# A hybrid decoder step: seven products in the FFN's down projection, 295 GB/s in the list scheduler's costs, one kind of weight sum kept as float32

## The chip, the cores and the metric

The kernel runs on one core of one Trainium2 chip. The metric is the device time of one execution in microseconds; the kernel before takes 2984.06 us, the median of three runs (2978.11 to 2984.43). Engines are named as in the profile: PE is TensorE, PEld its weight loads, DVE VectorE, ACT ScalarE, POOL GpSimd, SP the engine that issues DMAs.

## The reference

One layer of a hybrid decoder for a prompt of 2048 tokens and eight single decode tokens, in float32: a mixer (a convolution group beside gated DeltaNet), cross-attention into 256 memory tokens, and the dense FFN, to which the change belongs:

```python
def swiglu(h, w_gate, w_up, w_down):
    return (jax.nn.silu(h @ w_gate) * (h @ w_up)) @ w_down
...
x = x + swiglu(rms_norm(x, norm_ffn), w_gate, w_up, w_down)
```

The model width is 1024, the hidden width 2816.

## The kernel before

Channels lie on the 128 partitions and tokens run along the free axis. The prompt is cut into four blocks of 512 tokens; block 2 also carries the eight decode tokens in its FFN (520 columns, two halves of 260). The hidden width is 22 chunks of 128, called f; the model width is 8 chunks, called m.

Every float32 product is made of three matmuls. A weight tile w holds the value rounded to fp32r in its first half and the rest in its second; so do activations. `three` issues high x high, high x low and low x high into the same PSUM bank. The rounding is a ScalarE copy, the rest a subtraction on GpSimd or VectorE ("split"): `WS.split` does it for weights, choosing GpSimd unless it is behind.

The gate and up projections of a chunk f are already done in seven products (`product`: Q1, P5, P6, Q2, Q3, Q7, P4) of half a block's tokens each, in the banks fx, fy and fz, from four sums of weight tiles besides the tiles themselves. The sums are made once, split, and parked in DRAM (`sums`) as split pairs, 512 KB each; blocks 1 to 3 load them straight into a weight tile, without a split. `ff_split` multiplies the two branches (ffu, ffs) and splits the result into a tile ff.

The down projection (`down(g, j)`) takes a pair of chunks f and two of the eight m: for each m a bank dn gets 2 x 3 matmuls over all 512 tokens (in block 2 two banks of 260), and one VectorE addition brings the bank to the residual tile x. A pair and four j are one weight load of 256 KB and one split each.

`ffn_steps` lists the steps of one block, `ffn_plan` turns them into the order of weight loads and splits, `ffn` walks through them and records the instructions. Behind block 2's products the down projections of three pairs (`HOLD`) are kept back and stand between block 2's last product and block 3's first (`rest`): the bridge, in which block 3's norm is made.

What is recorded is not what is issued. `Tape.order` sorts all instructions again with a list scheduler: it keeps an own clock for each engine, with a cost for each kind (`Tape.cost`), latencies between engines (`LAT`), the buffers of each pool, and issues what is ready, the earliest needed first. Each engine then executes its own queue in that fixed order. A DMA's cost there is its bytes over a rate. Pools that matter here: six weight tiles (`NW`), eleven raw tiles (`NRAW`), 28 float32 tiles (`NT2`), 22 split activations (`NACT`), and for these products the PSUM banks of the tags mm, cv and o.

The line that the profile names is that of a recording helper for all instructions (L469), so rows are told apart by tile names: dn the down projection's banks, fx, fy, fz those of the gate and up products, ffu and ffs their evacuated parts, ff the split hidden tile, x the residual, w a weight tile, raw what was loaded for it, op the split operands of the FFN.

## Time and profile before

| | before |
|---|---|
| median of 3 runs | 2984.06 us |
| the profiled execution: time | 2980.41 us |
| its span | 2978.7 us |
| TensorE busy | 2922.9 us, 98% |
| weight loads | 2601.6 us, 87% |
| VectorE, ScalarE, GpSimd busy | 66%, 46%, 50% |
| DMA, mean of the span | 199 GB/s |

The span is the time from the first to the last instruction of the execution that was profiled, and lies 1.7 us below that execution's device time. A busy matmul in the profile is pipelined: the next begins before it ends, so a group's duration of one is longer than its pace. The pace is read from the chain of waits, in which each piece ends where the next begins. The FFN of block 1 runs from about 1770 to 2123 us, that of block 2 from 2270 to 2580, the bridge to 2625, and block 3's FFN to 2955.

### The profile page before, as it was taken

Reading aid. Unit: us, or ns where it says so; the run is one execution under the profiler, and the core shown is the slowest. Engines: PE = TensorE matmul, PEld = TensorE weight load, DVE = VectorE, ACT = ScalarE, POOL = GpSimd, SP = SyncE. Lnnn points to the kernel's source line nnn. Section 1 sums busy time; section 2 is a strip of 40 time slices with the busy share of each in tenths; the row PEclk is TensorE's granted clock in tenths of the full one; section 3 lists DMA queues with packets and bytes.
Section 4 is the critical chain, followed back from the end, with each engine's and each line's share of the span. In section 5 each row is a group of like instructions: output and inputs, shape, how many; then the busy total and the mean of one; then the engine's idle time right before and its main releaser. Section 6 shows DMA issues by size and latency. Waiting matters only on the chain.

```text
span 2978.7 us, 53399 instructions
## 1 busy us (share of the span) xinstructions
PE 2922.9 (98%) x18972; PEld 2601.6 (87%) x18972; DVE 1975.7 (66%) x3973; ACT 1373.8 (46%) x2854; POOL 1478.0 (50%) x1407
## 2 busy tenths in 40 slices
PE   9999999999999998999999999999999999999998
PEld 7999878887888887999988789988888999999997
DVE  8757798987684867957689874433775444664345
ACT  6543556455764545635554553333453232333233
POOL 3544545776656454548875124445503444344444
PEclk9999999999999999999999999999999999999999
DMA  6533435877773435766778767867526666676663
GB/s 213 158 96 106 130 110 163 262 239 255 225 224 112 140 101 162 253 190 222 256 251 273 252 210 244 262 227 241 176 93 233 208 223 214 213 245 216 223 220 134
DMA packets 361962, 593.89 MB, mean 199 GB/s; under 512 B 54016, under 2 KB 148544, under 8 KB 361680
## 3 DMA queue, kind: packets, MB, share of 16 engines
q1 hardware_dynamic: 361696, 590.47, 61.4%
q8 instruction: 151, 2.47, 0.3%
q14 instruction: 115, 0.94, 0.1%
HBM read 476.65 MB, written 114.27 MB: 198 GB/s over the span
## 4 chain that ended last, share of the span: by engine, by line
PE 76%; DVE 7%; issue 5%; DMA 5%; POOL 5%; ACT 2%; SPq 0%; POOLq 0%; DVEq 0%; ACTq 0%
PE dn L469 14%; PE hd L469 11%; PE fy L469 11%; PE rg L469 9%; PE fx L469 7%; PE fz L469 7%; PE sc L469 5%; POOL w L469 3%; DVE cacc L469 3%; PE pu L469 2%; PE glua L469 2%; PE glub L469 2%; DMA w<-sums 1%; PE pch L469 1%; PE po L469 1%
## 5 line engine op out<-in xcount | busy, mean ns | idle before, releaser
L469 POOL TENSOR_TENSOR w<-raw,w 128x512 fp32r<-128x512 f32 x709 | 957.4, 1361 | 877.7 <-ACT w L469 830.3
L469 ACT ACTIVATE w<-raw 128x512 fp32r<-128x512 f32 x912 | 568.6, 631 | 827.7 <-PE fx L469 175.0
L469 PE MATMUL dn<-ff,w 128*128 128x512 f32 (+2 forms) x2688 | 514.2, 347 | 0.8 <-DVE ffs L469 0.6
L469 PEld LDWEIGHTS dn<-ff,w 128*128 128x128 f32 x2688 | 422.8, 188 | 61.5 <-issue 0.8
L469 PE MATMUL fy<-op,w 128*128 128x256 f32 (+1 forms) x3168 | 426.5, 282 | 3.6 <-DMA w<-sums 3.5
L469 PEld LDWEIGHTS fy<-op,w 128*128 128x128 f32 x3168 | 398.6, 188 | 8.9 <-DVE ffu L469 2.8
L469 PE MATMUL hd<-hT,w 128*128 128x512 f32 (+2 forms) x1920 | 397.7, 357 | 8.2 <-ACT w L469 6.0
L469 DVE SCALAR_TENSOR_TENSOR cacc<-cu,cw,cacc 128x512 f32<-128x512 f32 x480 | 359.5, 749 | 16.1 <-ACT cacc L469 8.2
L469 PEld LDWEIGHTS hd<-hT,w 128*128 128x128 f32 x1920 | 304.3, 189 | 52.5 <-ACT w L469 6.8
L469 DVE TENSOR_TENSOR x<-dn,x 128x512 f32<-128x512 f32 (+1 forms) x448 | 254.4, 572 | 139.4 <-PE dn L469 136.1
L469 PE MATMUL fz<-op,w 128*128 128x256 f32 (+1 forms) x2112 | 287.4, 282 | 0.2 <-DMA w<-sums 0.2
L469 PE MATMUL fx<-op,w 128*128 128x256 f32 (+1 forms) x2112 | 284.7, 282 | 0.3
L469 PEld LDWEIGHTS fx<-op,w 128*128 128x128 f32 x2112 | 267.2, 189 | 6.9 <-issue 1.2
L469 PEld LDWEIGHTS fz<-op,w 128*128 128x128 f32 x2112 | 265.3, 188 | 2.2 <-issue 1.3
L469 POOL TENSOR_TENSOR sqj<-sqj,sqj 128x512 f32<-128x512 f32 (+1 forms) x98 | 134.1, 1368 | 265.5 <-ACT sqj L469 263.3
L469 DVE TENSOR_TENSOR w<-raw,w 128x512 fp32r<-128x512 f32 x203 | 180.0, 892 | 69.4 <-ACT w L469 66.0
L469 PE MATMUL rg<-pT,w 128*128 128x512 f32 x768 | 191.5, 401 | 8.1 <-ACT cres L469 7.9
L469 PE MATMUL sc<-w,hT 128*128 128x512 f32 x768 | 189.4, 398 | 2.4 <-DVE w L469 1.3
L469 PE MATMUL rg<-catS,w 128*128 128x512 f32 (+1 forms) x960 | 188.2, 352 | 1.8 <-ACT jn L469 1.7
L469 DVE TENSOR_TENSOR ffu<-fy,ffu 128x256 f32<-128x256 f32 (+1 forms) x176 | 74.4, 423 | 167.2 <-PE fy L469 167.2
L469 PEld LDWEIGHTS rg<-catS,w 128*128 128x128 f32 x960 | 154.4, 188 | 27.0 <-ACT jn L469 2.5
L469 PEld LDWEIGHTS rg<-pT,w 128*128 128x128 f32 x768 | 142.0, 190 | 40.7 <-ACT cres L469 8.3
(378 smaller groups left out, 4101.2 us busy)
## 6 DMA issues: line engine op xcount, KB each, us to landing
w<-sums SPq DMA_DIRECT2D x296, 512.0 KB, 4.5
raw<-in_w_gate_dram SPq DMA_DIRECT2D x192, 256.0 KB, 3.3
sums<-w SPq DMA_DIRECT2D x88, 512.0 KB, 4.1
raw<-in_w_down_dram SPq DMA_DIRECT2D x176, 256.0 KB, 3.0
raw<-in_w_up_dram SPq DMA_DIRECT2D x118, 256.0 KB, 2.9
raw<-in_w_in_dram SPq DMA_DIRECT2D x96, 256.0 KB, 3.1
raw<-in_w_out_dram SPq DMA_DIRECT2D x64, 256.0 KB, 4.3
raw<-wk SPq DMA_DIRECT2D x64, 256.0 KB, 2.9
```

The costliest lines, as they stand in the source:

```text
L469: fn(*args, **kw)
```

## The change

The down projection of the first twenty chunks f in blocks 1 to 3 is done in seven products of half a block's tokens. Two chunks f and two chunks m (now j and j + 4) make a 2 x 2 matrix of weight tiles, two chunks f and two halves of the tokens one of activations; four sums of the weights and four of the activations take the place of the eighth product (`sums_down`, `pair_split`). `downs(g, j)` does two pairs at once: 7 products x 2 pairs x 3 matmuls into three banks, dx, dy and dz, which are added to x after each product and go on accumulating. The last pair of chunks and all of block 0 stay with `down`, with m and the weight layout changed to j and j + 4. Block 1 makes the weight sums from `w_down` (128 columns each, in place in the raw tiles) and parks them in `dsums` as float32; blocks 2 and 3 load them from there, 512 and 384 columns, and split them.

The fourth sum of the gate and up weights (`WHOLE = (3,)`, the tile of Q7) is parked as float32 (256 KB, `sums1`) in place of a split pair (512 KB), and split whenever it is loaded. The list scheduler's DMA cost uses 295 in place of 360 bytes per ns. In block 2 the residual tiles hold the decode tokens beside each half until the last pair. Counted over the whole program, TensorE issues 600 instructions more (17942 before), VectorE 185 (3975), ScalarE 251 (2599), GpSimd 297 (1412) and SP 200 (1948).

```diff
-            return max(size / 360.0, 90.0), False, None
+            return max(size / 295.0, 90.0), False, None
...
+    def ffn_steps_ds(b):
+        steps = []
+        for f in range(NF):
+            if f == 0 or not early:
+                steps.append(("Q1", f))
+            dec = [w for w, (db, f0) in (("w_mq", DEC_Q), ("w_mo", DEC_O)) if db == b and f0 <= f < f0 + KC]
+            steps += [("P5", f), ("P6", f)]
+            steps += [("dec", dec[0], 2 * (f - (DEC_Q if dec[0] == "w_mq" else DEC_O)[1]) + n) for n in range(2) if dec]
+            steps += [("Q2", f), ("Q3", f), ("Q7", f)]
+            units = [[], []]
+            for g in range(NDS - (b == NB - 2)):
+                for j, (df, end) in enumerate(DS_AT):
+                    if f == min(4 * g + 4 + df, NF - 1):
+                        units[end].append(("downs", g, j))
+            early = not units[0] + units[1] and f + 1 < NF
+            if early:
+                steps.append(("Q1", f + 1))
+            steps += units[0] + [("P4", f)] + units[1]
+        if b < NB - 2:
+            steps += [("down", NG - 1, j) for j in range(KC // 2)]
+        return steps
+    def downs_plan(b, g, j):
+        if b > DS_B:
+            for n in range(2):
+                for p in (2 * g, 2 * g + 1):
+                    plan.append(("dsums", "s", (p, j), n))
+            return
+        raws = {}
+        for p in (2 * g, 2 * g + 1):
+            for n in (1, 0):
+                raws[p, n] = plan.raw("dma", "w_down", "h", (p, j), n)
+        for n in range(2):
+            for p in (2 * g, 2 * g + 1):
+                plan.append(("dsums", "s", (p, j), n), raws[p, n])
...
+    WHOLE = (3,)
...
+                elif PROD[st] in WHOLE:
+                    plan.append(ffn_key(st, f), plan.raw("dma", "sums1", "u", f, WHOLE.index(PROD[st])))
+                else:
+                    plan.append(ffn_key(st, f), -1)
...
-            plan.extend(("w_down", "d", g, j) for g in range(NG - HOLD, NG) for j in range(KC // 2))
+            for j in range(KC // 2):
+                downs_plan(b, NDS - 1, j)
+            plan.extend(("w_down", "d", NG - 1, j) for j in range(KC // 2))
...
+                elif kind == "h":
+                    at = b_ * TB // 2
+                    dma(r[:, at : at + TB // 2], src[a][:, at : at + TB // 2], fr)
+                elif kind == "s":
+                    wd = TB - b_ * P
+                    dma(r[:, :wd], src[a[0], a[1], b_, :, :wd], fr)
...
+                if n in WHOLE:
+                    dma(wsrc["sums1"][f, WHOLE.index(n)], r)
+                else:
+                    dma(wsrc["sums"][f, n], t.bitcast(F32))
...
+        def split_down(self, j, k, r, t):
+            _, _, at, n = plan[j]
+            wd = TB - n * P
+            if plan.raws[k][2] == "h" and n == 0:
+                self.sums_down(at, r, self.raw[k - 1])
+            A.activation(out=t[:, 0, :wd], in_=r[:, :wd], func=AF.Copy)
+            self.engine().tensor_tensor(out=t[:, 1, :wd], in0=r[:, :wd], in1=t[:, 0, :wd].bitcast(F32), op=ALU.subtract)
+            self.tiles[j] = t
+            self.sp += 1
+            self.used(k)
+        def sums_down(self, at, r0, r1):
+            (a11, a12, s1, s2), (s3, s4, a22, a21) = ([r[:, n * P : (n + 1) * P] for n in range(4)] for r in (r0, r1))
+            eng = self.engine(2600.0)
+            for out, x, y, op in (
+                (s1, a21, a22, ALU.add), (s2, s1, a11, ALU.subtract), (s3, a11, a21, ALU.subtract), (s4, a12, s2, ALU.subtract)
+            ):
+                eng.tensor_tensor(out=out, in0=x, in1=y, op=op)
+            p, j = at
+            dma(wsrc["dsums"][p, j, 0], r0)
+            dma(wsrc["dsums"][p, j, 1, :, : 3 * P], r1[:, : 3 * P])
...
+        def pair_split(p):
+            (u1, s1), (u2, s2) = prod.pop(2 * p), prod.pop(2 * p + 1)
+            half = lambda t, n: t[:, n * w : (n + 1) * w]
+            yield [u2, s2]
+            V.tensor_tensor(out=u2, in0=u2, in1=s2, op=ALU.mult)
+            V.tensor_tensor(out=half(s2, 1), in0=half(u2, 1), in1=half(u1, 1), op=ALU.subtract)
+            V.tensor_tensor(out=half(u1, 1), in0=half(u1, 1), in1=half(u1, 0), op=ALU.subtract)
+            V.tensor_tensor(out=half(s2, 0), in0=half(u2, 1), in1=half(u1, 1), op=ALU.subtract)
+            V.tensor_tensor(out=half(s1, 0), in0=half(u2, 0), in1=half(s2, 0), op=ALU.subtract)
+            for n, (src, wd) in enumerate(((u1, 2 * w), (u2, 2 * w), (s2, 2 * w), (s1, w))):
+                yield ("act", 1)
+                a = act("fo")
+                A.activation(out=a[:, 0, :wd], in_=src[:, :wd], func=AF.Copy)
+                yield a
+                V.tensor_tensor(out=a[:, 1, :wd], in0=src[:, :wd], in1=a[:, 0, :wd].bitcast(F32), op=ALU.subtract)
+                drop(src)
+                hx[p, n] = a
...
-                S.add(ff_split(f, u[:, : 2 * w], s_[:, : 2 * w]))
+                if b < DS_B or f >= 4 * NDS:
+                    S.add(ff_split(f, u[:, : 2 * w], s_[:, : 2 * w]))
+                else:
+                    prod[f] = u[:, : 2 * w], s_[:, : 2 * w]
+                    S.add(pair_split(f // 2) if f % 2 else ff_mult(f, *prod[f]))
...
+        def downs(g, j):
+            ps_ = (2 * g, 2 * g + 1)
+            S.until(lambda: all((p, n) in hx for p in ps_ for n in range(4)), "ff")
+            wts, bk = {}, {}
+            for n, at, (x, h), t, m, half in (
+                (0, 0, (0, 0), "x", j, 0), (0, 1, (1, 0), "y", j, 0), (0, 2, (0, 1), "z", j + 4, 1), (0, 3, (2, 0), "x", j, 1),
+                (1, 1, (1, 1), "z", j, 1), (1, 0, (2, 1), "x", j + 4, 1), (1, 2, (3, 0), "x", j + 4, 0),
+            ):
+                if (n, ps_[0]) not in wts:
+                    for p in ps_:
+                        wts[n, p] = [ws.get("dsums", "s", (p, j), n)]
+                first = t not in bk
+                if first:
+                    bk[t] = pm("d" + t, (P, w))
+                pt = bk[t]
+                for p in ps_:
+                    wt = wts[n, p]
+                    three([pt], wk(wt, 0, at), wk(wt, 1, at), hx[p, x], [(h * w, (h + 1) * w)], first and p == ps_[0], p == ps_[1], True)
+                    tick()
+                if at == (3, 2)[n]:
+                    ws.free(2)
+                lo, hi = half * w, (half + 1) * w
+                V.tensor_tensor(out=xs[m][:, lo:hi], in0=pt, in1=xs[m][:, lo:hi], op=ALU.add)
+            if j == KC // 2 - 1:
+                drop(*[hx.pop((p, n)) for p in ps_ for n in range(4)])
```

TensorE, block 3, the down projection of the first pairs: before: two m of one j, with the product P4 (fy) behind the first j. dn_5779 and dn_5780 are two banks, ff the split hidden tiles of two chunks f.

```order
L469 MATMUL dn_5779<-ff_5737,w_5765 128x512 x3
L469 MATMUL dn_5779<-ff_5768,w_5765 128x512 x3
L469 MATMUL dn_5780<-ff_5737,w_5765 128x512 x3
L469 MATMUL dn_5780<-ff_5768,w_5765 128x512 x3
L469 MATMUL fy_5771<-op_5527,w_5769 128x256 x3
```

The same place now, the first unit of one group and j = 0. fo are the split activation sums of two pairs.

```order
L474 MATMUL dx_5999<-fo_5943,w_5985 128x256 x3
L474 MATMUL dx_5999<-fo_5968,w_5988 128x256 x3
L474 MATMUL dy_6000<-fo_5944,w_5985 128x256 x3
L474 MATMUL dy_6000<-fo_5971,w_5988 128x256 x3
L474 MATMUL dx_5999<-fo_5945,w_5985 128x256 x3
L474 MATMUL dx_5999<-fo_5973,w_5988 128x256 x3
L474 MATMUL dz_6001<-fo_5943,w_5985 128x256 x3
L474 MATMUL dz_6001<-fo_5968,w_5988 128x256 x3
L474 MATMUL dx_5999<-fo_5945,w_5991 128x256 x3
L474 MATMUL dx_5999<-fo_5973,w_5993 128x256 x3
```

A bank was written once and left; now TensorE comes back to dx_5999 after six matmuls of another bank, with VectorE's read in between.

VectorE in block 3, before: the additions of a pair's banks to x, with the product's own reads among them.

```order
L469 TENSOR_TENSOR x_5511<-dn_5923,x_5511 128x512
L469 TENSOR_TENSOR x_5512<-dn_5924,x_5512 128x512
L469 TENSOR_TENSOR ffu_5907<-fy_5915,ffu_5907 128x256
L469 TENSOR_TENSOR ffu_5907<-ffu_5907,ffs_5908 128x512
L469 TENSOR_TENSOR x_5513<-dn_5928,x_5513 128x512
```

And now, the reads of the unit above and the beginning of the next, with an operation of `pair_split` (ffs from ffu and ffu) in the last row.

```order
L474 TENSOR_TENSOR x_5647<-dx_5999,x_5647 128x256
L474 TENSOR_TENSOR x_5647<-dy_6000,x_5647 128x256
L474 TENSOR_TENSOR x_5647<-dx_5999,x_5647 128x256
L474 TENSOR_TENSOR x_5651<-dz_6001,x_5651 128x256
L474 TENSOR_TENSOR x_5651<-dx_5999,x_5651 128x256
L474 TENSOR_TENSOR x_5647<-dz_6001,x_5647 128x256
L474 TENSOR_TENSOR x_5651<-dx_5999,x_5651 128x256
L474 TENSOR_TENSOR ffu_5983<-fy_5990,ffu_5983 128x256
L474 TENSOR_TENSOR ffu_5983<-ffu_5983,ffs_5984 128x512
L474 TENSOR_TENSOR x_5648<-dx_6010,x_5648 128x256
L474 TENSOR_TENSOR ffs_5984<-ffu_5983,ffu_5963 128x256
```

Seven reads of half the width stand where four of the full width stood for two pairs, and between the units' reads now stand sums of two tiles in SBUF.

GpSimd in block 1, now: splits of weight tiles (w) with the sums of down weights (raw on raw, 128 columns) among them; before, only splits of 512 columns stood there.

```order
L474 TENSOR_TENSOR w_4620<-raw_4599,w_4620 128x384
L474 TENSOR_TENSOR w_4629<-raw_4604,w_4629 128x512
L474 TENSOR_TENSOR raw_4614<-raw_4613 128x128
L474 TENSOR_TENSOR raw_4613<-raw_4614,raw_4613 128x128
L474 TENSOR_TENSOR raw_4614<-raw_4614 128x128
L474 TENSOR_TENSOR w_4631<-raw_4608,w_4631 128x512
L474 TENSOR_TENSOR w_4633<-raw_4610,w_4633 128x512
```

Counted over the block, GpSimd's splits go from 108 of 512 columns to 92 of 512 and 26 of 384, with 160 sums beside them, and VectorE's splits from 2 to 54.

## Rows read from the trace of the kernel before

**Rows 1.** The head of the page, the busy time of each engine (us, share of the span, instructions), and TensorE's granted clock in 40 slices (tenths of full speed).

```profile
span 2978.7 us, 53399 instructions
...
PE 2922.9 (98%) x18972; PEld 2601.6 (87%) x18972; DVE 1975.7 (66%) x3973; ACT 1373.8 (46%) x2854; POOL 1478.0 (50%) x1407
...
PEclk9999999999999999999999999999999999999999
```

**Rows 2.** Busy time of each engine in four stretches (instructions in brackets), with the granted clock, the share of the DMA engines and GB/s.

```profile
1770.00:2123.00 353.00, 350.17 (x2416) 320.36 (x2415) 159.42 (x276) 128.25 (x242) 167.93 (x128) 1.00 0.74 242
2270.00:2580.00 310.00, 308.99 (x2573) 308.62 (x2573) 147.19 (x429) 100.00 (x193) 132.38 (x98) 1.00 0.71 228
2580.00:2625.00 45.00, 44.86 (x384) 44.44 (x383) 42.03 (x130) 19.65 (x36) 17.95 (x14) 1.00 0.45 136
2625.00:2955.00 330.00, 329.39 (x2322) 307.98 (x2321) 142.73 (x249) 101.66 (x194) 146.51 (x109) 1.00 0.67 218
```

**Rows 3.** What TensorE waited for in the whole program: us in total, times, longest.

```profile
PE rg L469 <- ACT cres L469: 7.9, 1, 7.9
PE hd L469 <- ACT w L469: 6.0, 1, 6.0
...
PE fy L469 <- DMA w<-sums: 3.5, 6, 1.0
...
PE dn L469 <- DVE ffs L469: 0.6, 1, 0.6
...
PE dn L469 <- ACT ffs L469: 0.2, 1, 0.2
```

**Rows 4.** The chain of waits in order of time, block 3: start us, us to the next piece, what.

```profile
2904.62 8.31 PE dn L469 x36
2912.94 1.43 PE fx L469 x12
2914.37 1.42 PE fz L469 x12
```

**Rows 5.** The same in block 2.

```profile
2522.02 2.95 PE dn L469 x24
...
2526.41 8.66 PE dn L469 x72
2535.06 1.44 PE fx L469 x12
```

**Rows 6.** The timeline where the down projection waited for a bank, of TensorE and of VectorE: start us, us, instruction, idle time before it and what ended it.

```profile
2648.81 1.33 PE L469 MATMUL fz<-op,w 128*128 128x256 f32 x10
2650.75 0.93 PE L469 MATMUL dn<-ff,w 128*128 128x512 f32 x3 [0.61 <-DVE ffs L469]
...
2650.18 0.42 DVE L469 TENSOR_TENSOR ffs<-fz,ffs 128x256 f32<-128x256 f32 x1 [2.40 <-PE fz L469]
```

**Rows 7.** Groups of instructions with shapes kept apart, whole program: busy us, mean ns of one, then idle time before.

```profile
L469 PE MATMUL dn<-ff,w 128*128 128x512 f32 x1536 | 371.9, 395 | 0.8 <-DVE ffs L469 0.6 <-ACT ffs L469 0.2
L469 PE MATMUL fy<-op,w 128*128 128x256 f32 x2376 | 321.2, 282 | 2.6 <-DMA w<-sums 2.5
...
L469 PE MATMUL dn<-ff,w 128*128 128x260 f32 x1056 | 130.5, 283 | 0.0
...
L469 PE MATMUL fx<-op,w 128*128 128x260 f32 x528 | 70.8, 283 | 0.0
```

**Rows 8.** VectorE's operations by tile: duration of one in ns, least, median and most, first and last start. x from dn reads PSUM and SBUF, the others read two SBUF tiles.

```profile
L469 DVE TENSOR_TENSOR x<-dn,x x448: 406/677/693, 1227.2 to 2966.8; 128x512 f32<-128x512 f32 x85, 128x256 f32<-128x256 f32 x65
...
L469 DVE TENSOR_TENSOR ffu<-ffu,ffs x88: 674/693/1787, 1206.3 to 2946.1; 128x512 f32<-128x512 f32 x66, 128x520 f32<-128x520 f32 x22
...
L469 DVE TENSOR_TENSOR tt<-xn,xn x16: 408/417/1519, 1138.5 to 2605.5; 128x256 f32<-128x256 f32 x12, 128x260 f32<-128x260 f32 x4
```

**Rows 9.** Groups in the stretch from 2625 to 2955 us (block 3): busy us, mean ns of one, then idle time before.

```profile
L469 DVE TENSOR_TENSOR x<-dn,x 128x512 f32<-128x512 f32 x80 | 55.3, 692 | 46.3 <-PE dn L469 45.4
L469 DVE TENSOR_TENSOR ff<-ffu,ff 128x512 fp32r<-128x512 f32 x22 | 18.8, 855 | 0.2
L469 DVE TENSOR_TENSOR ffu<-fy,ffu 128x256 f32<-128x256 f32 x44 | 18.7, 424 | 55.8 <-PE fy L469 55.8
...
L469 POOL TENSOR_TENSOR w<-raw,w 128x512 fp32r<-128x512 f32 x107 | 145.2, 1370 | 178.9 <-ACT w L469 160.2 <-DMA w<-sums 12.2 <-DMA out_dram<-x 2.8
...
L469 ACT ACTIVATE w<-raw 128x512 fp32r<-128x512 f32 x106 | 66.9, 631 | 122.9 <-PE fx L469 64.6 <-PE fy L469 25.2 <-PE fz L469 20.7
```

**Rows 10.** GpSimd's smaller additions, whole program, same columns.

```profile
L469 POOL TENSOR_TENSOR bit<-biq,w 32x64 f32<-32x64 f32 x32 | 13.7, 437 | 7.3 <-DVE biq L469 7.0
...
L469 POOL TENSOR_TENSOR sqj<-sqj,sqj 128x256 f32<-128x256 f32 x8 | 5.9, 742 | 8.9 <-ACT sqj L469 8.5
```

**Rows 11.** VectorE's additions of the down projection in block 2 (2270 to 2625 us), same columns; xd is the decode tokens' residual.

```profile
L469 DVE TENSOR_TENSOR x<-dn,x 128x256 f32<-128x256 f32 x176 | 72.4, 417 | 28.7 <-PE dn L469 27.9
L469 DVE TENSOR_TENSOR xd<-dn,xd 128x4 f32<-128x4 f32 x176 | 26.0, 149 | 0.0
```

More of the change, by code (lines that the diff above doesn't have):

```diff
@@ L46 @@
 NG = NF // 2
+DS_B = 1
+NDS = 5
+DS_AT = ((1, 0), (1, 1), (2, 0), (2, 1))
 NW = 6
@@ L818, in ffn_plan @@
             elif b or any(f in fs for fs in SUMS_AT.values()):
-                plan.append(ffn_key(st, f), -1 if st in PROD else None)
+                if st not in PROD:
+                    plan.append(ffn_key(st, f))
+                elif PROD[st] in WHOLE:
+                    plan.append(ffn_key(st, f), plan.raw("dma", "sums1", "u", f, WHOLE.index(PROD[st])))
+                else:
+                    plan.append(ffn_key(st, f), -1)
             else:
@@ L961, in split @@
             r = self.raw[k]
+            if plan[j][0] == "dsums":
+                self.split_down(j, k, r, t)
+                return
             A.activation(out=t[:, 0, :], in_=r, func=AF.Copy)
@@ L969, in split @@
             eng.tensor_tensor(out=t[:, 1, :], in0=r, in1=t[:, 0, :].bitcast(F32), op=ALU.subtract)
-            if plan[j][0] == "sums":
+            if plan[j][0] == "sums" and plan.raws[k][0] == "sum":
                 _, _, f, n = plan[j]
-                dma(wsrc["sums"][f, n], t.bitcast(F32))
+                if n in WHOLE:
+                    dma(wsrc["sums1"][f, WHOLE.index(n)], r)
+                else:
+                    dma(wsrc["sums"][f, n], t.bitcast(F32))
             self.tiles[j] = t
@@ L975, in split @@
             self.used(k)
+        def split_down(self, j, k, r, t):
[18 more added lines that the diff above has]
+            dma(wsrc["dsums"][p, j, 1, :, : 3 * P], r1[:, : 3 * P])
         def ready(self, k):
+            if 0 <= k < self.ld and plan.raws[k][2] == "h" and plan.raws[k][4] == 0 and C.when([self.raw[k - 1]]) > S.vt:
+                return False
             return k < 0 or k < self.ld and C.when([self.raw[k]]) <= S.vt
@@ L1979, in hybrid_step @@
     wsrc["wk"] = dram.tile([1, D, D], F32, tag="wk", name="wk")
+    wsrc["sums1"] = dram.tile([NF, len(WHOLE), P, TB], F32, tag="sums1", name="sums1")
     wsrc["sums"] = dram.tile([NF, 4, P, 2, TB], F32, tag="sums", name="sums")
+    wsrc["dsums"] = dram.tile([2 * NDS, KC // 2, 2, P, TB], F32, tag="dsums", name="dsums")
     xpark = dram.tile([NB - 1, KC, P, TB], F32, tag="xpark", name="xpark")
@@ L2571, in ffn_norm @@
                 yield ("t2", 1 + RES)
-                xs[k] = t2("x")
-                dma(xs[k], xpark[b - 1, k])
+                xs[k] = t2("x", (P, 2 * w))
+                dma(halves(xs[k], w, TB // 2), xpark[b - 1, k].rearrange("p (n t) -> p n t", n=2))
         if b == DEC_F:
             yield lambda: dec_lanes["f"][0] is None
+            for k in range(KC):
+                V.tensor_copy(out=halves(xs[k], w)[:, :, TB // 2 :], in_=xd[:, k, :].rearrange("p (n d) -> p n d", n=2))
         def parts_of(a, src, lo=None):
@@ L2587, in ffn_norm @@
                 V.scalar_tensor_tensor(
-                    out=halves(x, w, TB // 2), in0=halves(xs[kc], TB // 2), scalar=vcol("norm_ffn", kc),
+                    out=halves(x, w, TB // 2), in0=halves(xs[kc], w, TB // 2), scalar=vcol("norm_ffn", kc),
                     in1=halves(rsb, TB // 2), op0=ALU.mult, op1=ALU.mult,
@@ L2631, in ffn, with ff_mult @@
         hact, hold = {}, {}
-        bank = {}
+        bank, prod, hx = {}, {}, {}
+        def pair_split(p):
[15 more added lines that the diff above has]
+                hx[p, n] = a
+        def ff_mult(f, u, s_):
+            yield [u, s_]
+            V.tensor_tensor(out=u, in0=u, in1=s_, op=ALU.mult)
         def ff_split(f, u, s_):
@@ L2694, in ffn, with add_half @@
                 S.add(finish_last(xs, fin, *span, n_ == 1))
-        def add_half(m, pts):
+        def add_half(m, pts, last):
+            x = xs[m]
+            if last:
+                need("t2", 1)
+                xs[m] = t2("x")
             for n_, pt in enumerate(pts):
-                lo, hi = n_ * TB // 2, (n_ + 1) * TB // 2
-                V.tensor_tensor(out=xs[m][:, lo:hi], in0=pt[:, : TB // 2], in1=xs[m][:, lo:hi], op=ALU.add)
-                if w > TB // 2:
+                lo, hi = n_ * w, (n_ + 1) * w
+                if last:
+                    mid, at = lo + TB // 2, n_ * TB // 2
+                    V.tensor_tensor(out=xs[m][:, at : at + TB // 2], in0=pt[:, : TB // 2], in1=x[:, lo:mid], op=ALU.add)
@@ L2701, in add_half @@
                     dx = xd[:, m, n_ * DEC // 2 : (n_ + 1) * DEC // 2]
-                    V.tensor_tensor(out=dx, in0=pt[:, TB // 2 :], in1=dx, op=ALU.add)
+                    V.tensor_tensor(out=dx, in0=pt[:, TB // 2 :], in1=x[:, mid:hi], op=ALU.add)
+                else:
+                    V.tensor_tensor(out=x[:, lo:hi], in0=pt, in1=x[:, lo:hi], op=ALU.add)
+            if last:
+                drop(x)
+        def downs(g, j):
[23 more added lines that the diff above has]
+                drop(*[hx.pop((p, n)) for p in ps_ for n in range(4)])
@@ L2726, in rest @@
         def rest():
-            for g in range(NG - HOLD, NG):
-                for j in range(KC // 2):
-                    down(g, j)
+            for j in range(KC // 2):
+                downs(NDS - 1, j)
+            for j in range(KC // 2):
+                down(NG - 1, j)
             if b == DEC_F:
@@ L2740, in last @@
                     for n_, f in enumerate(fs):
[L2741 to L2742 removed]
+                        at = n_ if m < 4 else 3 - n_
+                        three([pt], wk([wts[m % 4]], 0, at), wk([wts[m % 4]], 1, at), hact[f], [(lo, hi)], n_ == 0, n_ == 1)
                         tick()
@@ L2853, in lay_out @@
     out["w_mqT"] = inp["w_mq"].transpose(0, 2, 1)
-    wd = inp["w_down"][0].reshape(NG, 2, P, KC // 2, 2, P)
-    out["w_down"] = wd.transpose(0, 3, 2, 4, 1, 5).reshape(NG, KC // 2, P, TB)
+    wd = inp["w_down"][0].reshape(NG, 2, P, 2, KC // 2, P).transpose(0, 4, 2, 3, 1, 5).copy()
+    wd[:, :, :, 1] = wd[:, :, :, 1, ::-1].copy()
+    out["w_down"] = wd.reshape(NG, KC // 2, P, TB)
     return {k: np.ascontiguousarray(v) for k, v in out.items()}
```

18 lines of the change are left out of this document (11 added, 7 removed).

## The prediction

> **What bounds the kernel now.** I read the page's head first: TensorE is busy for 98% of the span at full granted clock, VectorE for 66%, GpSimd for 50%, ScalarE for 46% [rows 1]. Then the table of stretches, to see whether this holds where the change sits: in the FFN of block 1 (1770 to 2123 us), of block 2 (2270 to 2580), the bridge behind it (2580 to 2625) and in block 3 (2625 to 2955) TensorE is busy for 99% or more [rows 2]. Then the list of what TensorE waited for: transfers of weight sums cost 3.5 us in six waits of the whole program, and the down projection waited for a bank twice, 0.6 and 0.2 us [rows 3]. So the end is set by the sum of TensorE's own paces, and the chain of waits gives these, start to start: 36 matmuls of 512 columns in 8.31 us, 0.2308 us each; 12 of 256 in 1.42 us, 0.1183 each [rows 4]; in block 2, 96 of 260 columns in the down projection in 11.61 us, 0.1209 each, and in the gate and up products 12 in 1.44 us, 0.1200 each [rows 5].
>
> **The products themselves.** For one pair of hidden chunks and one j the old code issues 12 matmuls of 512 columns (24 of 260 in block 2); the new one issues 7 products of 3, so 21 of half the width. Ten of eleven pairs, four j and three blocks are changed. Blocks 1 and 3: 2 x 480 = 960 matmuls go, 960 x 0.2308 = 221.6 us; 2 x 840 = 1680 come, 1680 x 0.1183 = 198.7 us; gain 22.9. Block 2: 960 x 0.1209 = 116.1 go, 840 x 0.1200 = 100.8 come; gain 15.3. Together 38.2 us, all on the path, since nothing but TensorE is near its limit there.
>
> A rule speaks against such a trade. The row is 0.2308 us at 512 columns and 0.1183 at 256, so nearly all of a matmul's pace is columns [rows 4]. The Trainium skill ("TensorE: Matmul & The Clock Gate", Back-to-back issue gap) gives for a stream of weight loads and matmuls about 131 ns at 512 columns and 81 at 128; on a straight line, as an estimate from that page, 256 would take 98 ns, and blocks 1 and 3 would lose 38 us and block 2 gain 12. The trace disagrees at 512 columns by 100 ns, and the measurement decides.
>
> **Turns of a bank.** The old down projection reads each PSUM bank once. The new one adds a bank to x, lets TensorE go on accumulating into the same bank, and reads it again: bank dx four times, dz twice, so four turns in a unit (one j of one group of two pairs), 60 units, 240 turns. Behind a waiting matmul stands all of TensorE's queue. A bare turn is in the trace: the fz matmuls end at 2648.81 + 1.33 = 2650.14, VectorE's read runs from 2650.18 to 2650.60, the next matmul on the bank starts at 2650.75 [rows 6]. One matmul lasts 0.28 us [rows 7], so the last fz began at 2649.86; to 2650.75 are 0.89 us, and with its own slot of 0.12 taken off 0.77 us must be filled by other matmuls. In the order of the changed kernel the filling is six matmuls (0.71 us) or less at 84 of the 240 turns, seven or eight at 53, more at the others. So 84 x 0.06 = 5 us are lost if VectorE reads at once. This is the lower end; if each read came 0.33 us late (need 1.1 us) the same count over the order gives 43 us. I take 5, by the bare turn, and 3 for lateness.
>
> **VectorE, ScalarE.** Per pair: four half-width sums (0.42 us each, as the 256-column adds) and splits of 3.5 tiles for 2. In block 3: 80 adds of 512 at 0.692 go (55 us), 140 of 256 at 0.424 come (59); 20 splits at 0.855 go (17), 40 sums and 30 + 10 splits come (17 + 26 + 4) [rows 9]. That is 34 us on top of 142.7 [rows 2], 177 of some 320, so it lies beside TensorE; where a read comes late it is priced above. ScalarE gets 62 more weight copies (22 full at 0.631, 40 of 384 columns, about 0.5) and 15 more of the products: 44 us on 101.7 of 330 [rows 2, 9]. Beside TensorE too.
>
> **Weights.** The fourth sum of each f (22 in each of blocks 1 to 3, 8 in block 0) is now loaded as 256 KB of float32 and split again, and each pair and j of blocks 1 to 3 has two tiles to split (512 and 384 columns) where there was one. Block 3: GpSimd's splits go from 108 to 127 full ones and 40 of 384 columns; a full one costs 1.370 us [rows 9], one of 384 about 1.06, between 0.742 at 256 [rows 10] and 1.370. So 174 + 42 = 216 us for 148, of some 320: hidden on the average. But two units and one product follow each other: 9 tiles, 5 x 1.37 + 4 x 1.06 = 11.1 us of GpSimd against 84 x 0.1183 + 1.42 = 11.4 us of TensorE. Six tiles may stand ready ahead, so I cost blocks 2 and 3 at nothing. In block 1 GpSimd also makes the sums: 16 small ones in such a burst, each between 0.437 (32 x 64) and 0.742 us (128 x 256) [rows 10], say 0.5: 8 us more, 19 against 11.4. VectorE takes 54 of the block's 172 splits by the order, and the raw tiles allow work ahead; none (0) to all of it (77 us over ten bursts) is possible; I take 4, near the lower end, because GpSimd was idle for half of that stretch (168 of 353) [rows 2].
>
> **Transfers.** 74 reads and 22 writes of 512 KB become 256 KB, 25 MB less; the new tensor adds 40 x 448 KB written and 80 x 192 KB more read, 33 MB: 8 MB more on balance. Shares of 0.67 to 0.74 of the queues [rows 2] stay as they are. The lower rate in the scheduler's costs moves loads earlier in its plan, so the 3.5 us of waits for sums [rows 3] may go: between 0 and -4, I take -1. It also reshuffles the first 1190 us, where TensorE's long waits are (7.9 and 6.0 us [rows 3]); those depend on ScalarE, not on transfers: 0, with 5 to either side.
>
> **The bridge.** Between block 2's last P4 and block 3's first product TensorE had 12 units of 24 matmuls, 34.8 us, and waited next to nothing while VectorE was busy for 42 of 45 us [rows 2]. Now it has 4 x 42 x 0.12 + 4 x 24 x 0.1209 = 31.8 us. VectorE's adds there shrink too: from 48 x 0.417 + 48 x 0.149 = 27 us to 28 x 0.42 + 16 x 0.417 + 16 x 0.149 = 21 [rows 11]. Cover and covered both shrink: 0, at most 3.
>
> **Sum.** -38.2 + 5 + 3 + 4 - 1 = -27 us on the profiled execution's 2980.4: 2953. The median of the runs shown is 3.7 us above that execution, within their spread of 6; I say 2954.
>
> **Rivals.** (a) *Late turns.* VectorE reads the banks late because its queue holds operations that wait for GpSimd. For it: an operation with two SBUF inputs lasts 0.693 us as a rule but up to 1.787 [rows 8], and pair_split adds such ones right between the adds; against it: adds out of PSUM never lasted more than 0.693 [rows 8], and TensorE's waits for VectorE are tiny where VectorE was as full as this (the bridge). At a need of 1.1 us the turns cost 43 instead of 8 us: 2953 + 35 = 2988; at 1.0 us 29: 2974. The Trainium skill ("GPSIMD Engine Reference", 1. Specifications) says that GpSimd shares its SBUF interfaces with VectorE, in contention with VectorE's instructions of two SBUF inputs; the trace agrees, and by that rule more GpSimd work makes this rival likelier.
> (b) *Slower: GpSimd in the bursts of block 1.* Tiles come later than TensorE wants them, and it waits at each first matmul of a tile. It cancels the net gain from 2.7 us a burst on; at half of the 7.7 us by which it is short, plus the like of 0.2 in the other 20 bursts, 10 x 3.9 + 4 - 4 = 39: 2992 and more. Against it: half of GpSimd idle, no wait of TensorE for a split in this stretch before.
> (c) *A half-width matmul costs more than half.* By busy time over count, 371.9 / 1536 = 0.242 for 512, 130.5 / 1056 = 0.124 in block 2's old form, 0.135 for 256 and 0.134 for 260 with a bank of its own [rows 7]: 351 us go, 340 come, gain 11: 2969 without any loss, 2980 with the 11 above. Busy time here counts overlapping ends twice at changes of group, so I give it little. The extreme of it, by the page named in the second part, is a loss of 27 us, 3018 with the 11; the row at 512 columns leaves that no chance of its own.
> (d) *The order gains beyond the products*, transfers' and early waits vanishing: 2938 to 2945.
>
> **How the numbers follow.** Forecast 0.62, its own range 2940 to 2968; (a) 0.16; (b) 0.10; (c) 0.06; (d) 0.06. A range from 2936 to 2990 leaves out (b) and the ends of (a) and (d), under 2 in 10. What this kernel's runs can tell from no change is 0.2%, 6 us. Faster: 0.62, 0.06 of (d), 0.04 of (c) and 0.03 of (a), 0.75; same: 0.08 of (a) and 0.02 of (c), 0.10; slower: (b) and 0.05 of (a), 0.15.
>
> **What would show it.** Right: TensorE's groups dx, dy, dz with 2520 matmuls and some 0.118 us from start to start in the chain; waits of TensorE for VectorE's x adds of a few hundredths each, 5 to 10 us in all; VectorE and GpSimd at 55 to 75% in blocks 1 to 3. Wrong: waits of TensorE for w (ScalarE or GpSimd) of microseconds around 1770 to 2120, or a list of waits in which x from dx or dz adds up to tens of microseconds.

## The result and the profile after

| | before | after |
|---|---|---|
| median of 4 runs | 2984.16 us | 2962.91 us (2957.16 to 2966.44) |
| ratio, 95% interval | | 0.9932 [0.9914, 0.9949] |
| the profiled execution: time, span | 2980.41, 2978.7 us | 2966.44, 2964.7 us |
| TensorE's own paces, summed | 2868.9 us | 2830.1 us |
| TensorE's stalls over them, before 1700 us | 79.9 us | 69.4 us |
| the same, from 1700 us on | 16.4 us | 52.5 us |

The time fell by 21.3 us on the medians, 14.0 on the two profiled executions (the one of after is the slowest of its four). The last three rows are counted from the starts of all matmuls in a trace: a shape's pace is its median time from start to start in the kernel before, a stall is what a step takes beyond it. With the first matmul's start (6.0 us in both) and the tail (7.4 and 6.8 us) they add up to the span.

The head of the page of after, as [rows 1]:

```profile
span 2964.7 us, 55974 instructions
...
PE 2908.8 (98%) x19572; PEld 2617.8 (88%) x19572; DVE 2140.7 (72%) x4158; ACT 1491.9 (50%) x3105; POOL 1737.5 (59%) x1704
```

The stretches that answer to [rows 2], block 1, block 2, bridge and block 3, same columns:

```profile
1758.00:2104.00 346.00, 335.57 (x2734) 324.32 (x2733) 241.73 (x426) 161.00 (x312) 267.86 (x289) 1.00 0.84 276
2263.00:2574.00 311.00, 309.70 (x2552) 307.99 (x2551) 178.06 (x346) 138.84 (x273) 197.82 (x155) 1.00 0.74 234
2574.00:2612.00 38.00, 34.42 (x257) 33.48 (x256) 35.86 (x91) 18.54 (x34) 12.78 (x10) 0.91 0.53 159
2612.00:2952.00 340.00, 337.35 (x2810) 334.82 (x2809) 204.99 (x395) 149.59 (x299) 224.11 (x182) 1.00 0.70 221
```

TensorE was busy for 99% or more of all four; now it is for 97% of block 1 and 91% of the bridge, where the granted clock is no longer 1.00. GpSimd went from 48% to 77% of block 1. What TensorE waited for in the whole program, as [rows 3]:

```profile
PE hd L474 <- ACT w L474: 6.5, 2, 6.0
PE fy L474 <- DMA w<-sums: 4.7, 4, 2.0
PE fz L474 <- DMA w<-sums: 3.9, 7, 2.0
...
PE dn L474 <- DVE xd L474: 2.5, 3, 1.1
PE fx L474 <- ACT ffs L474: 2.3, 2, 1.8
...
PE dx L474 <- DVE x L474: 0.8, 1, 0.8
```

The 7.9 us of rg for ScalarE's cres are gone; the waits for weight sums have grown. The view lists only gaps above a threshold; the many stalls of some 0.1 us at bank turns are seen in the counted stalls alone. The chain of waits in block 3, as [rows 4], with one of those waits for sums in it:

```profile
2699.88 0.71 PE dx L474 x6
2700.59 0.71 PE dy L474 x6
2701.30 0.71 PE dz L474 x6
...
2703.06 0.03 PE dz L474
2703.09 6.55 DMA w<-sums
2709.65 0.14 issue
2709.78 1.65 PE fy L474 x12
```

Six matmuls in 0.71 us are 0.118 each, as the prediction had it. Each such group of six takes three from one weight tile and three from another; by the order of TensorE a tile of a unit comes back in four or three groups, so it lasts 12 or 9 matmuls, not the six that one of the expectations below names. The load of a weight sum went out at 2703.09, landed 6.55 us later, and TensorE, which had work up to 2707.8, waited 2.0 us for it.

### The profile page after: what moved, and what is told of

Read it like the earlier page. It is cut to its first block, busy times and chain, and to the rows that moved or that the text cites. A ratio compares the mean times of both kernels' runs of the same rounds, so it can differ in the third digit from the quotient of the medians.

```text
span 2964.7 us, 55974 instructions
## 1 busy us (share of the span) xinstructions
PE 2908.8 (98%) x19572; PEld 2617.8 (88%) x19572; DVE 2140.7 (72%) x4158; ACT 1491.9 (50%) x3105; POOL 1737.5 (59%) x1704
## 5 line engine op out<-in xcount | busy, mean ns | idle before, releaser
L474 POOL TENSOR_TENSOR w<-raw,w 128x512 fp32r<-128x512 f32 (+1 forms) x846 | 1115.1, 1330 | 665.7 <-ACT w L474 601.5
L474 ACT ACTIVATE w<-raw 128x512 fp32r<-128x512 f32 (+1 forms) x1106 | 668.5, 618 | 866.3 <-PE rg L474 103.5
L474 PE MATMUL fx<-op,w 128*128 128x256 f32 (+1 forms) x2112 | 296.4, 282 | 2.3 <-ACT ffs L474 2.3
L474 DVE TENSOR_TENSOR w<-raw,w 128x512 fp32r<-128x512 f32 x260 | 224.9, 871 | 81.2 <-ACT w L474 76.9
L474 PE MATMUL dx<-fo,w 128*128 128x256 f32 (+1 forms) x1440 | 216.7, 286 | 0.9 <-DVE x L474 0.8
L474 PEld LDWEIGHTS dx<-fo,w 128*128 128x128 f32 x1440 | 186.8, 188 | 4.1 <-DVE x L474 1.7
L474 PE MATMUL rg<-catS,w 128*128 128x512 f32 (+2 forms) x960 | 188.3, 352 | 0.0
L474 PE MATMUL dn<-ff,w 128*128 128x512 f32 (+2 forms) x768 | 172.8, 374 | 4.5 <-DVE xd L474 2.5
L474 PEld LDWEIGHTS sc<-w,hT 128*128 128x128 f32 x768 | 142.5, 189 | 35.2 <-ACT pr L474 2.1
```

Source lines behind the costliest of these rows:

```text
L474: fn(*args, **kw)
```

## Experiments

All ratios are to the kernel before, run beside it on the same chip. From 1700 us on, the counted stalls are shown by what ended them. "Short leads" is counted from TensorE's recorded order with its paces: for each sum loaded straight into a weight tile in blocks 1 to 3, the time from the last use of the sixth tile before it (when its place is free) to its first use; how many are under 5 us.

| kernel | ratio, 95% | paces | stalls to 1700 | from 1700 | waits for sums | bank turns | short leads |
|---|---|---|---|---|---|---|---|
| before | 1 | 2868.9 | 79.9 | 16.4 | 5.2 | 0 | 0 |
| rate | 0.9954 [0.9942, 0.9967] | 2868.9 | 74.3 | 11.6 | 1.9 | 0 | 0 |
| float32 sum | 0.9973 [0.9961, 0.9984] | 2868.9 | 76.7 | 12.9 | 1.5 | 0 | 1 |
| rate, float32 sum | 0.9940 [0.9922, 0.9957] | 2868.9 | 71.1 | 9.4 | 0.2 | 0 | 1 |
| seven | 1.0033 [1.0020, 1.0045] | 2830.1 | 81.8 | 67.4 | 31.6 | 7.9 | 33 |
| seven, rate | 1.0019 [1.0008, 1.0030] | 2830.1 | 80.2 | 63.4 | 12.5 | 10.0 | 29 |
| seven, float32 sum | 0.9977 [0.9968, 0.9986] | 2830.1 | 78.1 | 56.3 | 18.5 | 7.4 | 33 |
| all three (after) | 0.9932 [0.9914, 0.9949] | 2830.1 | 69.4 | 52.5 | 12.5 | 8.4 | 27 |

The last column alone does not order the waits for sums: 33 short leads stand beside 31.6 us of them and beside 18.5, 29 beside 12.5. What else counts is said behind the experiments, under *Transfers*.

**Each part alone, and two together.** The first four kernels were the kernel before with the rate alone, with the float32 sum alone, and the changed kernel with the old rate, with and without the float32 sum.

```diff
-            return max(size / 360.0, 90.0), False, None
+            return max(size / 295.0, 90.0), False, None
```

> The kernel before with 295 in place of 360 in the scheduler's DMA cost, nothing else. Theory A (the changed kernel gains its products' 38.9 us of pace and gives some 18 back at places that the seven products make: bank turns, weight tiles, the bridge): the rate only reshuffles, within 6 us of 2984, ratio 0.998 to 1.002. Rival B (the rate itself moves loads so that TensorE gains in the first 1180 us, where the changed kernel's trace lost 12.8 us less): 2970 to 2976, ratio 0.995 to 0.997. Rival C (the rate is what lengthens the waits for weight sums from 5 to 12 us): 2988 to 2992, ratio over 1.001, and those waits at 10 us or more in the trace.

Measured: 2968.32 us against 2981.38, a ratio that B gave and a time below B's. B had the gain in the first 1180 us; by the table 5.6 us of stalls go before 1700 us and 4.8 behind.

```diff
+    WHOLE = (3,)
...
+                elif PROD[st] in WHOLE:
+                    plan.append(ffn_key(st, f), plan.raw("dma", "sums1", "u", f, WHOLE.index(PROD[st])))
```

> The kernel before with the fourth sum of the gate and up weights parked as float32 and split when loaded, nothing else. Theory A: 62 more splits lie beside TensorE; 24 MB less traffic and one direct load less per f shorten the waits for weight sums (5.3 us before) to 2 to 4: 2978 to 2984. Rival (the splits on GpSimd and ScalarE come late): 2988 or more, with waits of TensorE for w from ACT or POOL.

Measured: 2973.79 us, faster than either theory had it; waits for sums fell to 1.5 us.

Against the changed kernel, the seven products alone:

```diff
-            return max(size / 295.0, 90.0), False, None
+            return max(size / 360.0, 90.0), False, None
...
-    WHOLE = (3,)
+    WHOLE = ()
```

> The changed kernel with 360 in the scheduler and all four gate and up sums as split pairs: the seven products alone. Theory A (the waits for weight sums come from the units, whose four weight tiles at a time leave the direct loads fewer of the six): waits for sums 12 us or more, more than with the fourth sum as float32; gain over the kernel before 12 to 20 us, 2964 to 2972. Rival B (the rate gives the gain of the first 1180 us): 2972 to 2980. Rival D (the products alone give all of it and the two others nothing): 2960 to 2965, waits for sums as in the changed kernel.

Measured: 2991.41 us, slower than before and than any of the three had it, though with the waits for sums that A gave (31.6 us, 12 or more). Its waits of TensorE:

```profile
PE fy L474 <- DMA w<-sums: 13.4, 13, 2.1
PE fz L474 <- DMA w<-sums: 11.4, 15, 1.5
PE rg L474 <- ACT cres L474: 7.9, 1, 7.9
```

The paces fell by the 38.9 us that were forecast, and 51 us came back as stalls from 1700 us on. Against the changed kernel, the old rate alone:

```diff
-            return max(size / 295.0, 90.0), False, None
+            return max(size / 360.0, 90.0), False, None
```

> The changed kernel with 360 in the scheduler, the fourth sum as float32. Theory A: within 6 us of the changed kernel's 2963. Rival B or C (the rate matters): B 2970 to 2976; C 2955 to 2958, with waits for weight sums near the 5 us of the kernel before.

Measured: 2974.11 us, in B's range: the rate matters. With the seven products the float32 sum is worth 0.56%, alone 0.27%: it takes a quarter of the sums off the direct loads.

**The other two pairs.**

```diff
-    WHOLE = (3,)
+    WHOLE = ()
```

> Seven products and the rate of 295, all four weight sums kept as split pairs. Theory A (the three parts add up as they did alone: +10.0 for the seven products, -13.1 for the rate): 2978 to 2981 us, with TensorE's waits for w from the sums still near the 24.8 us that the seven products had alone. Theory B (the rate is what brings the loads of sums forward, so it takes away the waits that the seven products made): 2962 to 2969, waits for w from the sums under 10 us.

Measured: 2987.45 us; neither range held. The waits for sums fell to 12.5 us, but by the count splits, turns and the operations between the products' banks took 32.5 where the seven products alone had 21.2.

```diff
-        if b >= DS_B:
-            return ffn_steps_ds(b)
```

(and all that this calls; the down projection as before)

> The rate of 295 and the float32 sum, with the old down projection. Theory A (the two gains add up: -13.1 and -7.6 against the kernel before): 2959 to 2962 us, and the seven products are worth nothing on top of them. Theory B (both cure the same early waits of TensorE, so the gains overlap): 2965 to 2970, and the seven products are worth 3 to 8 us on top. Theory C (the 38 us of the products come through once loads are in time): 2980 or more.

Measured: 2963.95 us, between A and B; C falls. Without the seven products the kernel is within 0.08% of the changed one, inside both intervals (each ratio is to the kernel before on its own chip). In the FFN blocks (1760 to 2960 us) its TensorE waits for nothing of note:

```profile
PE pss L469 <- DVE sqj L469: 3.5, 1, 3.5
PE fz L469 <- ACT ffu L469: 1.1, 1, 1.1
PE prs L469 <- POOL rs L469: 1.0, 1, 1.0
```

So the seven products bring 38.9 us of pace and cost 43.1 us of stalls from 1700 us on (52.5 against 9.4). The change's gain does not come from them.

**Where the first 1700 us gain.** In every kernel here with all four sums as split pairs rg waits 7.9 us for cres; in those with the float32 sum it waits 0.7 us at most. ScalarE's one operation that makes cres, in the kernel before and in the changed one (duration of one, first and last start):

```profile
L469 ACT ACTIVATE cres<-cacc x1: 579/579/579, 1152.9 to 1152.9; 128x512 f32<-128x512 f32 x1
```

```profile
L474 ACT ACTIVATE cres<-cacc x1: 597/597/597, 1131.9 to 1131.9; 128x512 f32<-128x512 f32 x1
```

The order puts it 21 us earlier; nothing about the operation itself has changed. Other waits take back part of it: with the float32 sum alone the stalls before 1700 us fall by 3.2 us only (79.9 to 76.7).

**Is it the lead or the queues?** A seventh weight tile, paid for with two of the 28 float32 tiles, and its control.

```diff
-NW = 6
-NT2 = 28
+NW = 7
+NT2 = 26
```

> The changed kernel with seven weight tiles in place of six, paid for with two of the 28 float32 tiles; to be read against the next kernel, which gives up the same two tiles and gets nothing. Theory A (a weight tile lasts six matmuls, 0.71 us, in the seven products, so a sum that is loaded straight into one of six tiles is issued only 4 to 4.7 us ahead and lands after 4.2 to 6.8): one tile more gives the load 0.7 to 1.4 us more, TensorE's waits for w from the sums fall from 8.6 us to under 4, and the time is 5 to 10 us below the next kernel's. Theory B (the loads are late because the queues are full): waits and time as in the next kernel within 3 us.

> The changed kernel with 26 float32 tiles in place of 28, the control for the kernel with seven weight tiles. Both theories: 2963 to 2972 us, waits of TensorE for w from the sums 8 to 12 us.

Measured: 3188.54 and 3008.43 us (ratios 1.0693 and 1.0094), far outside what either theory gave. With two float32 tiles less the order before the FFN is another: the control stalls 115 us before 1700, and with seven weight tiles TensorE waits in the DeltaNet stage:

```profile
PE pu L474 <- DMA Tm<-zt: 75.4, 4, 19.7
PE pod L474 <- ACT osc L474: 33.6, 5, 13.1
```

The times answer nothing. In the blocks of the FFN the waits for sums are 1.7 us with seven tiles and 5.6 with six, as A has it; but the changed kernel, with six tiles too, has 12.5, so the order alone can halve them.

**The old form in block 1.**

```diff
-DS_B = 1
+DS_B = 2
```

> The changed kernel with the old down projection in block 1 too; block 2 makes and parks the weight sums, block 3 loads them. From the traces of the changed kernel and of its like without the seven products, TensorE's stalls over its own paces in 1700 to 2125 us are 25.7 against 2.6 us, while block 1's share of the pace gained is 11.5. Theory A (making the sums is what hurts in block 1, and block 2 with its longer matmuls bears it better): block 1 comes back to stalls under 5 us, block 2 goes from 5 to at most 12; 2948 to 2958 us. Theory B (the stalls go with the making of sums, wherever that is): block 2 takes over 20 us or more; 2960 to 2970.

Measured: 2970.37 us, ratio 0.9973 [0.9961, 0.9985]. Block 1 comes back to 1.4 us of stalls in 1760 to 2125 (18.4 in the changed kernel), as A said; block 2 takes on 14.0 for 5.1, and the bridge 14.0 for 7.9, by one wait:

```profile
PE dn L474 <- ACT ff L474: 8.9, 1, 8.9
```

The time lies just above B's range. Neither theory had the wait in the bridge; that it makes the difference is argued from these stalls.

**Other sums kept as float32.**

```diff
-    WHOLE = (3,)
+    WHOLE = (2, 3)
```

> The changed kernel with two kinds of sums (the third and the fourth, both multiplied into the bank fz) kept as float32 and split when loaded, so only fy's two are loaded straight into a weight tile. Theory A (loads straight into one of six weight tiles come late): TensorE's waits of fz for sums go (6.8 us of stalls to under 1), those of fy stay at 4 to 7; 2953 to 2962 us. Theory B (22 more tiles to split in a block is too much for GpSimd, VectorE and ScalarE): waits for w from POOL, DVE or ACT of over 5 us in 1770 to 2125; 2965 or more.

The expectation had a bank wrong: the third sum goes into fz with the first, the fourth into fy with the second, so one direct load of each is left; the next expectation has the first sum's bank wrong likewise. Measured: 2987.09 us, 1.0034 [1.0021, 1.0046]. Waits for sums fall to 5.1 us (11 short leads), as A wants; splits cost 6.1 in place of 3.3. The time is lost elsewhere: 91.3 us of stalls before 1700 us against 69.4, and 16.6 at turns, where VectorE now comes late in block 1:

```profile
PE dx L474 <- DVE x L474: 4.8, 6, 1.2
...
PE fz L474 <- DMA w<-sums: 2.0, 2, 1.1
```

```diff
-    WHOLE = (3,)
+    WHOLE = (0, 3)
```

> The changed kernel with the first sum (multiplied into fy right behind a unit of seven products) and the fourth kept as float32. Theory A: TensorE's stalls of fy for sums fall from 5.7 us to under 3, those of fz stay at 5 to 8; 2954 to 2962 us. Theory B as for the kernel before this: over 5 us of waits for splits, 2965 or more. Both: the order of the first 1190 us is drawn anew by the other tiles of block 0, and may add or take up to 8 us that has nothing to do with either.

Measured: 2995.05 us, 1.0059 [1.0044, 1.0073]. Waits for sums 11.2 us: fy's stay (4.8), fz's are 6.4. A's picture of the place was wrong: by the count some 20 leads are still short, and nearly all of them are the third sum's, into fz. Before 1700 us stalls are 90.8, much more than the 8 us that were allowed for. Both kernels show how far a change in tiles of block 0 moves that part.

**Leads and bursts against each other.** TensorE's order is that of the changed kernel up to the FFN of block 1.

```diff
-DS_AT = ((1, 0), (1, 1), (2, 0), (2, 1))
+DS_AT = ((1, 1), (1, 1), (1, 1), (1, 1))
```

> The changed kernel with the four units of a group one behind the other at one chunk, in place of two at each of two chunks; TensorE's order is that of the changed kernel up to block 1's first units, so the first 1700 us are not drawn anew. Counted over the order of TensorE with its paces (0.118, 0.120 and 0.231 us), the time between the last use of the sixth weight tile before and the first use of a tile loaded straight from the sums is under 5 us at 11 loads; at 27 in the changed kernel, 33 with the seven products alone, 1 with the rate and the float32 sum alone, none in the kernel before. Theory A (that lead decides, since such a load lands 4 to 7 us after its issue): TensorE's stalls for w from the sums in 1760 to 2950 us fall from 12.5 to between 3 and 6 us, the turns of banks stay at 7 to 11, and the time is 2954 to 2960 us. Theory B (what is late are GpSimd's splits and sums in bursts, and SP behind them): four units in a row double the burst, waits for w from the sums or from splits in block 1 grow to 20 us or more, and the time is 2966 to 2985.

Measured: 2980.80 us, 1.0007 [0.9997, 1.0016], so 0.75% slower than the changed kernel; the profiled execution took 2977.41. Waits of TensorE from 1760 us on:

```profile
PE fy L474 <- DVE ffs L474: 4.7, 7, 0.7
PE fz L474 <- DMA w<-sums: 4.0, 6, 1.1
PE dx L474 <- DVE x L474: 3.5, 8, 1.4
PE dx L474 <- POOL w L474: 2.7, 4, 0.7
...
PE fx L474 <- POOL w L474: 1.0, 2, 0.7
```

Both theories hold in part. With 11 short leads in place of 27 the waits for sums fall from 12.5 to 6.8 us, and in block 1 from 7.8 to nothing, although loads there land no sooner (5.2 us as the median in both kernels): there the lead decides. But longer bursts bring stalls for splits (15.5 us for 3.3), for VectorE between the products' banks (15.8 for 9.1) and at turns (10.9 for 8.4). Time is B's, but not its 20 us of waits in block 1. No version that was run beats the changed kernel.

## Why the prediction was right in its number and wrong in its reasons

The time of 2962.91 us lies in the likeliest case's own range (2940 to 2968), but it came about in another way.

*The products themselves*: right in size. Forecast 38.2 us, counted 38.9; 960 + 480 matmuls dx, 480 + 240 dz and 240 + 120 dy are the 2520 that were named. Rival (c), and the page of the Trainium skill behind its extreme ("TensorE: Matmul & The Clock Gate", Back-to-back issue gap), fall: a step of 256 columns lasts 0.118 us in the seven products as it did before. What was wrong is the half sentence "all on the path, since nothing but TensorE is near its limit there". It was read from averages over blocks; what ran out were a buffer's lead and VectorE's time over a few microseconds.

*Turns of a bank*: right. 5 + 3 us forecast, 8.4 counted in the FFN. Rival (a) falls by this sum, and the adds out of PSUM never took longer than 430 ns. VectorE's operations in the changed kernel (least, median, most in ns):

```profile
L474 DVE TENSOR_TENSOR ffu<-ffu,ffs x88: 674/753/3051, 1197.6 to 2930.6; 128x512 f32<-128x512 f32 x66, 128x520 f32<-128x520 f32 x22
...
L474 DVE TENSOR_TENSOR ffs<-ffu,ffs x30: 408/1185/1518, 1788.2 to 2907.9; 128x256 f32<-128x256 f32 x20, 128x260 f32<-128x260 f32 x10
...
L474 DVE TENSOR_TENSOR x<-dx,x x240: 408/424/430, 1822.2 to 2941.4; 128x256 f32<-128x256 f32 x80, 128x260 f32<-128x260 f32 x40
```

*VectorE, ScalarE*: mis-sized. Block 3 was to have 177 us of VectorE in 320 and has 205 in 340, mostly because the sums of activations, costed at 0.42 us, take some 0.9 there and up to 1.5 in the program. ScalarE, 146 forecast, has 150. "Lies beside TensorE" fails by 6.5 us: stalls at fx, fy and fz for the operations that free them rose from 2.6 to 9.1.

*Weights*: right in size by coincidence. Stalls for splits are 3.3 us against 4 forecast, but the 4 were meant for the bursts of block 1, where the trace has 0.1; two single waits for a split on VectorE, one ahead of the FFN and one in the bridge, make most of the 3.3. Rival (b) did not come. (The 168 of 353 us that the prediction takes for GpSimd's idle time are its busy time [rows 2]; it was idle for 185.) GpSimd from 1760 to 2960 us, in the kernel before, in that with the rate and the float32 sum alone, and in the changed one (the fifth busy time):

```profile
1760.00:2960.00 1200.00, 1195.37 (x8461) 1114.65 (x8460) 594.37 (x1274) 425.59 (x812) 505.76 (x378) 1.00 0.66 214
```

```profile
1760.00:2960.00 1200.00, 1189.62 (x8446) 1110.63 (x8444) 610.88 (x1301) 463.78 (x882) 588.30 (x440) 1.00 0.63 199
```

```profile
1760.00:2960.00 1200.00, 1175.99 (x9086) 1129.84 (x9084) 780.92 (x1481) 545.02 (x1066) 746.64 (x671) 1.00 0.72 228
```

*Transfers*: the step that failed. "The 3.5 us of waits for sums may go" was argued from the load on the queues; by the count these waits were 5.2 us, and they went to 12.5, with the seven products alone to 31.6. Two things were missed, the lead and the place of the new traffic.

The lead: a direct load goes out when its tile is free. In the old down projection a tile lasted 12 matmuls of 512 columns or 24 of half the width, 2.8 to 2.9 us, and no lead was under 5 us; a unit of seven products goes through four tiles in 42 matmuls, 5.0 us, and frees them two at a time, and 27 to 33 leads are under 5 us. The traffic: that the shares of 0.67 to 0.74 "stay as they are" fails in block 1, where all the new sums are written. Its share went from 0.74 to 0.84, and a direct load takes longer to land; from 1770 to 2120 us in the kernel before and in the changed one (number, size, median us from issue to landing):

```profile
w<-sums SPq DMA_DIRECT2D x84, 512.0 KB, 4.3
```

```profile
w<-sums SPq DMA_DIRECT2D x60, 512.0 KB, 5.2
```

The longest took 7.9 and 8.1. In blocks 2 and 3 the medians stay (4.5 and 4.2 before, 4.4 and 4.3 now).

By the starts in the trace these shortest leads are a small part of the loss: only some 2 of the 12.5 us stand at loads with a lead under 5 us, and the load in the chain of block 3 had 5.1. Some 8 us are lost in block 1, where 23 of 66 loads also went out more than 1 us after their place was free (none of 88 before). There the waits go with the leads under 6 us: 23 of them and 19 us with the seven products alone, 12 and 3.7 us with the rate beside them, 6 and nothing with four units in a row, with landing medians of 5.2 to 5.8 in all three. The changed kernel has 11 such leads. How its 8 us divide between shorter leads, later issues and slower landings was not separated.

The Trainium skill ("DMA: Bandwidth & Descriptors", Anatomy of one DMA) has any wait for a semaphore done by the issuing sequencer before the dispatch; the chain of block 3 shown above agrees, its load goes out at the end of a dz matmul. One of the signs named for "wrong", waits for w of microseconds in 1770 to 2120, did come, from a DMA and not from ScalarE or GpSimd.

The other half of the step, "those depend on ScalarE, not on transfers: 0", failed too: the reshuffle of the part before 1700 us took 10.5 us off, with the wait for cres, 7.9 us, gone in it. ScalarE was rightly named, but what set the wait was its place in the order. This is rival (d), an order that gains beyond the products, beside losses which that rival did not have.

*The bridge*: forecast 0, at most 3; it stalls 7.9 us for 1.2. VectorE was busy for 94% of it, and TensorE waited for its adds and for one split; some 2.2 us are half a clock (last section). By the timeline of TensorE:

```profile
2599.28 0.48 PE L474 MATMUL dn<-ff,w 128*128 128x260 f32 x2 [0.93 <-DVE xd L474]
2600.25 0.51 PE L474 MATMUL dn<-ff,w 128*128 128x260 f32 x2 [0.49 <-DVE xd L474]
2601.84 1.38 PE L474 MATMUL dn<-ff,w 128*128 128x260 f32 x8 [1.09 <-DVE w L474]
2604.28 2.07 PE L474 MATMUL dn<-ff,w 128*128 128x260 f32 x8 [1.06 <-DVE xd L474]
```

Cover shrank and what it was to cover did not: VectorE's operations for the norm stood between the adds.

*Sum*: -38.9 of pace, +36.1 of stalls from 1700 us on, -10.5 before, -0.7 at the tail make the -14.0 of the profiled executions. The forecast had -38.2, +11 and 0. Losses 25 us too small met a gain in the early part that was put at 0 with 5 to either side. So the number was right by luck, by two errors that cancel in part, and the sentence on what the change is worth was wrong: by the kernel without them, the seven products are worth nothing that can be told here, and the 0.6% are the rate's and the float32 sum's. Whether the rate is better as a cost or only draws another order stays open: it gains 0.46% alone, 0.14% beside the seven products, 0.33% beside the float32 sum, 0.45% beside both, and no third value was tried.

## What to carry to other kernels

Before matmuls are traded for shorter ones, go through the issued order: for each load straight into a weight tile, count the time from when its place is free to its first use. Set it against the longest landings where the queues are fullest (5 to 8 us here), and not against their median or the average share. Where a scheduler draws the order, run the change without its main part: an edit of a constant moved other stages by 10 to 20 us here, as much as the edit that was meant. Averages over a block can't show that cover suffices over five microseconds.

## What was not expected of the hardware

Half a clock in the bridge. In stretches of 2.5 us of the changed kernel (TensorE's busy time is the second number, the granted clock the third from the end):

```profile
2595.00:2597.50 2.50, 2.50 (x23) 2.50 (x23) 2.50 (x10) 1.92 (x4) 0.00 (x0) 1.00 0.77 243
2597.50:2600.00 2.50, 1.32 (x10) 0.93 (x8) 2.50 (x7) 0.81 (x2) 0.00 (x0) 1.00 0.47 184
2600.00:2602.50 2.50, 1.17 (x7) 0.96 (x8) 2.50 (x8) 1.76 (x4) 0.00 (x0) 1.00 0.00 0
2602.50:2605.00 2.50, 1.44 (x8) 1.17 (x7) 2.50 (x10) 1.65 (x4) 0.13 (x1) 0.55 0.43 105
2605.00:2607.50 2.50, 2.50 (x14) 2.50 (x13) 1.96 (x6) 1.16 (x2) 2.19 (x2) 0.50 0.00 0
```

After two stretches in which it was busy for about half, TensorE was granted 0.50, the lower of its two levels (1.2 GHz), from 2602.7 to 2609.5 us. From 2604.6 to 2609.6 us a step of 260 columns took 0.217 us in place of 0.120, so 23 matmuls cost 2.2 us on top of the 3.6 us of the four waits in the timeline above. From 1700 us to the tail the changed kernel has 10.2 us at the half clock, the kernel before and that with the rate and the float32 sum none.

VectorE's operations with two SBUF inputs took up to 3.05 us in the changed kernel, 1.79 before [rows 8], while its adds out of PSUM kept their 0.42. The Trainium skill ("GPSIMD Engine Reference", 1. Specifications) says that GpSimd shares its SBUF interfaces with VectorE and contends with such instructions; this trace agrees, with GpSimd at 747 us for 506 in the blocks concerned.
